# Activations of a two-layer decoder kernel stored as even and odd token rows, read in turn by every product

## The chip, the cores and the metric

The kernel runs on one core of a Trainium2 chip. The metric is the device time of one execution in microseconds (us); lower is better. Shown times of the kernel before are the median of three runs; the profile is of one more execution, with a time of its own.

## The reference

Two layers of a decoder on 272 tokens (16 learned meta tokens and 256 of the sequence), width 2048. Cut to what matters:

```python
def hybrid_layer(h, pos, norm_g, w_in, conv_w, conv_b, gn_g, w_branch, w_out):
    u = rms_norm(h, norm_g)
    proj = jnp.einsum('bld,de->ble', u, w_in)            # 2048 -> 18432 columns
    q, k, v, g_ret, c_x, c_pre, c_post, g_conv, m_ret, m_conv = split_columns(proj)
    ...
    y_ret = head_group_norm(retention_chunkwise(q, k, v), gn_g)
    y_ret = jnp.einsum('blc,cd->bld', y_ret * silu(g_ret), w_branch[0])
    z = causal_depthwise_conv(c_pre * c_x, conv_w, conv_b)
    y_conv = jnp.einsum('blc,cd->bld', (c_post * z) * silu(g_conv), w_branch[1])
    merged = sigmoid(m_ret) * y_ret + sigmoid(m_conv) * y_conv
    return h + jnp.einsum('bld,de->ble', merged, w_out)
```

All of it is float32. The 16 meta tokens are dropped after the last norm.

## The kernel before

Activations stand transposed: 128 partitions hold 128 channels, and tokens run along the free dimension. A vector of 2048 channels is 16 such pieces (`KC`, index `k`). A product of float32 accuracy is made of fp32r products: every weight `w` and every activation `a` is split into a high part and the rest (`wh`, `wl`, and the two rows of `act`), and `wh*ah + wh*al + wl*ah` is summed in PSUM.

The two activation tiles are `pair[0]` and `pair[1]` (`act` in the trace; lines 65, 384), 16 pieces times two rows (high, low) of 272 floats, 1088 bytes a row. They are written by `gain_input` (lines 168 to 173, the norm's gain), and by `split_act` (lines 154 to 158), always with one ACT instruction for the high row and one DVE instruction for the low row. They are read by TensorE alone, as the moving operand, in `product` (lines 124 to 151) and in the opening (line 478).

The work is a list of blocks, one per 128 output channels: 128 columns of a weight matrix against all 16 pieces of `u` or `y`. SP loads a block's weights two blocks ahead in two halves of 512 KB; ACT writes `wh` (line 117) and DVE `wl` (line 118) from them. The order of the blocks is the order in which the program lists them: in each layer 8 retention heads (6 blocks each), 16 merge gates, 16 blocks of `w_br[0]`, 16 convolution groups of 4, 16 merge gates, 16 of `w_br[1]`, 16 of `w_out`. The first four blocks are computed together in the opening, while the input arrives.

`product` has two forms. In layer 0 all 272 tokens are needed, and a piece takes three matmuls of 272 columns (line 148). In layer 1 most blocks need 256 tokens: high and low rows fit into one PSUM bank side by side, so a piece takes one matmul of 512 columns for `wh` (line 133) and one of 256 for `wl` (line 136), and ACT and DVE add the two halves (lines 141, 142). Some blocks of layer 1 stay in the first form, with 272 columns (keys and values) or 258 (the convolution inputs, which start two tokens early); the last block of all has it with 256.

```python
nc.tensor.matmul(
    both, wh[:, o:o + P], mov[:, k, :, c0:L], start=(k == 0), stop=False, skip_group_check=True
)
nc.tensor.matmul(
    ps[:, :n], wl[:, o:o + P], mov[:, k, 0, c0:L],
    start=False, stop=(k == KC - 1), skip_group_check=True,
)
```

Of the kernel before, what the change touches and what calls it, by code (L numbers as in the profile page):

```python
# [10 lines left out]
F32R = mybir.dt.float32r  # L11
# [7 lines left out]
L = SEQ + META  # L19
DEPTH = 2  # L20
P = 128
KC = D // P
# [23 lines left out]
def hybrid_trunk(ctx: ExitStack, tc: tile.TileContext, xT, w_first, w_in, w_br, w_out, gains, params, consts, dec, outT):  # L46
# [3 lines left out]
    act = ctx.enter_context(tc.tile_pool(name="act", bufs=1))  # L50
# [6 lines left out]
    def f32(t):  # L57
        return t.bitcast(F32)

    def new(name, cols=L):  # L60
        return tmp.tile([P, cols], F32, tag="t", name=name, padded_shape=[P, L])


    h = act.tile([P, KC, L], F32, name="h")
    pair = [act.tile([P, KC, 2, L], F32R, name=f"act{i}") for i in range(2)]
    ss = act.tile([P, L], F32, name="ss")
    sums = act.tile([P, 2, L], F32, name="sums")

# [23 lines left out]
    def norm_gain(layer, k):  # L92
        return gain[:, layer * KC + k:layer * KC + k + 1]
# [14 lines left out]
    def load(src, cols, queue=nc.sync):  # L108
        full = [P, HALF * P]
        raw = rawp.tile([P, cols], F32, name="raw", padded_shape=full)  # L110
        queue.dma_start(raw, src)
        wh = whp.tile([P, cols], F32R, name="wh", padded_shape=full)
        wl = wlp.tile([P, cols], F32R, name="wl", padded_shape=full)
        return raw, wh, wl

    def cut(raw, wh, wl):
        nc.scalar.copy(wh, raw)  # L117
        nc.vector.tensor_tensor(out=wl, in0=raw, in1=f32(wh), op=ALU.subtract)  # L118
        return wh, wl

    def split(src):
        return [cut(*load(src[:, j * HALF * P:(j + 1) * HALF * P], HALF * P)) for j in range(2)]

    def product(parts, mov, c0, spare=False, narrow=False):
        n = L - c0
        ps = psr.tile([P, 512], F32, name="pr") if spare else psm.tile([P, 512], F32, name="ps")
        if 2 * n <= 512 and not narrow:

            both = ps.rearrange("p (s n) -> p s n", s=2)
            for k in range(KC):  # L130
                wh, wl = parts[k // HALF]
                o = (k % HALF) * P
                nc.tensor.matmul(  # L133
                    both, wh[:, o:o + P], mov[:, k, :, c0:L], start=(k == 0), stop=False, skip_group_check=True
                )
                nc.tensor.matmul(  # L136
                    ps[:, :n], wl[:, o:o + P], mov[:, k, 0, c0:L],
                    start=False, stop=(k == KC - 1), skip_group_check=True,
                )
            b, a = new("pb", n), new("pa", n)  # L140
            nc.scalar.copy(b, ps[:, n:])  # L141
            nc.vector.tensor_tensor(out=a, in0=ps[:, :n], in1=b, op=ALU.add)  # L142
            return a
        for k in range(KC):
            wh, wl = parts[k // HALF]
            o = (k % HALF) * P
            for i, (w, m) in enumerate(((wh, 0), (wh, 1), (wl, 0))):
                nc.tensor.matmul(  # L148
                    ps[:, :n], w[:, o:o + P], mov[:, k, m, c0:L],
                    start=(k == 0 and i == 0), stop=(k == KC - 1 and i == 2),  # L150
                )
        return ps[:, :n]

    def split_act(dst, k, c0, src):

        hi, lo = dst[:, k, 0, c0:L], dst[:, k, 1, c0:L]
        nc.scalar.copy(hi, src)
        nc.vector.tensor_tensor(out=lo, in0=src, in1=f32(hi), op=ALU.subtract)  # L158

# [3 lines left out]
    def norm_input(layer, dst, k, c0):  # L163

        gain_input(layer, dst, k, c0)
        sum_squares(k, c0)

    def gain_input(layer, dst, k, c0):
        g = norm_gain(layer, k)
        hk = h[:, k, c0:L]  # L170
        hi, lo = dst[:, k, 0, c0:L], dst[:, k, 1, c0:L]
        nc.scalar.activation(hi, hk, AF.Copy, scale=g)
        nc.vector.scalar_tensor_tensor(out=lo, in0=hk, scalar=g, in1=f32(hi), op0=ALU.mult, op1=ALU.subtract)

# [50 lines left out]
    def retention(layer, hd, i0, u, y):  # L225
# [85 lines left out]
        def normed():  # L311
            ps = psr.tile([P, 512], F32, name="pr")[:, :L - i0]
            for i, part in enumerate(st["sq"]):
                nc.tensor.matmul(ps, onesr, part, start=(i == 0), stop=(i == 1))  # L314
            sd, rg = new("ysd", L - i0), new("rg", L - i0)
            nc.scalar.activation(sd, ps, AF.Sqrt, bias=eps)  # L316
            nc.vector.reciprocal(rg, sd)  # L317
            for c in range(2):
                a = new("yn", L - i0)
                tt(a, st["y", c], rg)  # L320
                tt(a, a, st["g", c])
                split_act(y, 2 * hd + c, i0, a)
# [24 lines left out]
    def conv(layer, k, i0, u, y):  # L347
# [30 lines left out]
        def cpost(ps):  # L378
            a = new("yc", L - i0)
            tt(a, ps, st["g"])  # L380
            split_act(y, k, i0, a)
# [9 lines left out]
    for layer in range(DEPTH):  # L391
# [23 lines left out]
        def merge(k):  # L415
            def done(ps, acc=acc, gm=gm, u=u, i0=i0):
                tt(gm[k], ps, gm[k])
                tt(acc[k], acc[k], gm[k], ALU.add)
                split_act(u, k, i0, acc[k])
            return done  # L420
# [31 lines left out]
    pss = [psm.tile([P, 512], F32, name="ps") for _ in range(FIRST)]  # L452
# [6 lines left out]
    for k0, nk in START:  # L459
        cols = FIRST * nk * P  # L460
        src = w_first[:, k0 * FIRST * P:(k0 + nk) * FIRST * P]
        ks = range(k0, k0 + nk)
        nc.sync.dma_start(h[:, k0:k0 + nk, :], xT[:, k0:k0 + nk, :])  # L463
        raw, wh, wl = load(src, cols, nc.sync if k0 else nc.scalar)
        if k0 == 0:
            nc.scalar.activation(warm, eps, AF.Sqrt)
            nc.vector.tensor_copy(wh, raw)
        for k in ks:
            gain_input(0, pair[0], k, 0)
        if k0 > 0:  # L470
            nc.scalar.copy(wh, raw)
        nc.vector.tensor_tensor(out=wl, in0=raw, in1=f32(wh), op=ALU.subtract)
        nc.scalar.activation(squares[:, k0:k0 + nk, :], h[:, k0:k0 + nk, :], AF.Square)
        for w, m in ((wh, 0), (wh, 1), (wl, 0)):
            for n in range(FIRST):
                for k in ks:
                    o = ((k - k0) * FIRST + n) * P
                    nc.tensor.matmul(  # L478
                        pss[n][:, :L], w[:, o:o + P], pair[0][:, k, m, :],
                        start=(k == 0 and w is wh and m == 0), stop=(k == KC - 1 and w is wl),  # L480
                    )
        if k0 == 2:
            for z in zp:
                nc.gpsimd.memset(z, 0.0)
# [4 lines left out]
    n = KC  # L489
# [9 lines left out]
    for b, (_, mov, c0, done) in list(enumerate(blocks))[FIRST:]:  # L499
        ps = product(ready.pop(b), mov, c0, spare=(b < FIRST + 2), narrow=(b == len(blocks) - 1))  # L500
        if b + 2 < len(blocks):
            ready[b + 2] = split(blocks[b + 2][0])
        if b == FIRST:
            layer_scales((sums[:, 0, :], sums[:, 1, :]))
            for i in range(FIRST):
                blocks[i][3](pss[i][:, :L])
        for fn in hooks.get(b, ()):
            fn()
        done(ps)
# [3 lines left out]
    for j in range(2):  # L513
        c = slice(META + j * half, META + (j + 1) * half)
        token_scale(c, (ss[:, c], sq[:, j * half:(j + 1) * half]))
        for i, (k, n, eng) in enumerate(FINAL):
            hk = h[:, k:k + n, c]
# [78 lines left out]
```

## Time and profile before

| | |
|---|---|
| median of three runs | 2325.72 us (2325.2 to 2325.87) |
| profiled execution: time | 2325.07 us |
| its span, first to last instruction | 2323.3 us |
| mean granted TensorE clock over the span | 0.998 |
| TensorE matmuls busy | 2308.6 us (99%), 16761 instructions |
| weight loads (PEld) busy | 2210.2 us (95%) |
| VectorE (DVE) busy | 1473.4 us (63%) |
| ScalarE (ACT) busy | 1061.8 us (46%) |
| read from HBM | 409.40 MB, 177 GB/s over the span |

The profiled execution's own time is 1.8 us over its span and 0.65 us under the median. A busy TensorE is not a TensorE at its peak: matmuls are pipelined, and the mean duration of one in the trace (287 ns for 272 columns) is longer than the distance from one to the next. What a matmul costs is read from the distance between starts, or from the length of a run of matmuls in the chain of work divided by their number.

### The profile page before, as it was taken

To read this page: it belongs to the slowest core of one execution; us is meant where nothing else is said; L and a number is where in the kernel's file an instruction comes from. 1 tells how busy PE (TensorE), PEld (TensorE's weight loads), DVE (VectorE), ACT (ScalarE), POOL (GpSimd) and SP (SyncE) were. 2 spreads that over 40 slices of the span, in tenths; PEclk is the share of its full clock that TensorE was granted. 3 is DMA by queue.
4 is the path that set the end of the run, shared out by engine and by line. 5 is a ranking of instruction groups with operands and counts; after the bars stand their busy time and mean duration, and the time that the engine had idled before them with its cause. 6 is when DMAs were issued, how large, how long until landed. Compare 5 with 4: busy or idle time off the path is not lost.

```text
span 2323.3 us, 40412 instructions
## 1 busy us (share of the span) xinstructions
PE 2308.6 (99%) x16761; PEld 2210.2 (95%) x16761; DVE 1473.4 (63%) x2046; ACT 1061.8 (46%) x1470; POOL 48.3 (2%) x52
## 2 busy tenths in 40 slices
PE   9999999999999999999999999999999999999997
PEld 9999999999999999999999999988899999988886
DVE  8767664446666565455667777755566666656765
ACT  6555553333333333444445555544444444444443
POOL 0000000000000000000100000000000000000012
PEclk9999999999999999999999999999999999999999
DMA  7555555555555555555555555455555555555553
GB/s 280 164 165 168 166 170 177 174 177 176 175 178 174 176 177 174 177 177 174 178 175 171 174 170 174 161 190 185 188 184 186 186 182 189 183 187 185 188 183 108
DMA packets 119177, 414.13 MB, mean 178 GB/s; under 512 B 13008, under 2 KB 19536, under 8 KB 118992
## 3 DMA queue, kind: packets, MB, share of 16 engines
q1 hardware_dynamic: 116224, 409.97, 54.4%
q8 instruction: 131, 2.15, 0.4%
q10 hardware_dynamic: 2768, 1.57, 0.2%
q14 instruction: 54, 0.44, 0.0%
HBM read 409.40 MB, written 2.10 MB: 177 GB/s over the span
## 4 chain that ended last, share of the span: by engine, by line
PE 99%; DVE 0%; DMA 0%; SPq 0%; ACT 0%; DVEq 0%; issue 0%; ACTq 0%
PE ps L148 62%; PE ps L133 22%; PE ps L136 11%; PE ps L478 1%; PE pr L223 1%; PE pr L300 1%; PE pr L148 1%; PE pr L280 0%; PE pr L268 0%; DMA raw<-in_w_first 0%; PE pr L314 0%; DVE h L519 0%; PE pr L197 0%; DVE rs L200 0%; DVEq L591 0%; SPq L463 0%
## 5 line engine op out<-in xcount | busy, mean ns | idle before, releaser
L148 PE MATMUL ps<-act,wh 128*128 128x272 f32 (+1 forms) x7776 | 1453.3, 287 | 0.0
L117 ACT CAST wh<-raw 128x1024 fp32r<-128x1024 f32 x760 | 798.7, 1051 | 1166.7 <-PE ps L148 557.6
L118 DVE TENSOR_TENSOR wl<-raw,wh 128x1024 fp32r<-128x1024 f32 x760 | 929.7, 1224 | 617.2 <-ACT wh L117 613.2
L148 PEld LDWEIGHTS ps<-act,wh 128*128 128x128 f32 x7776 | 1217.2, 188 | 0.8
L148 PE MATMUL ps<-act,wl 128*128 128x272 f32 (+1 forms) x3888 | 1118.0, 288 | 0.0
L133 PE MATMUL ps<-act,wh 128*128 128x512 f32 x2160 | 765.3, 395 | 0.0
L148 PEld LDWEIGHTS ps<-act,wl 128*128 128x128 f32 x3888 | 732.8, 188 | 0.0
L136 PE MATMUL ps<-act,wl 128*128 128x256 f32 x2160 | 611.8, 283 | 0.0
L133 PEld LDWEIGHTS ps<-act,wh 128*128 128x128 f32 x2160 | 405.6, 188 | 94.5 <-DVE act L158 0.3
L136 PEld LDWEIGHTS ps<-act,wl 128*128 128x128 f32 x2160 | 406.9, 188 | 0.1
L188 POOL TENSOR_TENSOR ss<-ss,sq 128x272 f32<-128x272 f32 (+1 forms) x28 | 32.7, 1166 | 1640.2 <-ACT sq L181 1640.2
L142 DVE TENSOR_TENSOR pa<-ps,pb 128x256 f32<-128x256 f32 x135 | 56.4, 418 | 5.0 <-ACT pb L141 5.0
L141 ACT COPY pb<-ps 128x256 f32<-128x256 f32 x135 | 49.4, 366 | 5.5 <-PE ps L136 5.5
L161 DVE TENSOR_TENSOR gs<-ps,rs 128x272 f32<-128x272 f32 x62 | 27.3, 440 | 35.9 <-PE ps L148 35.9
L317 DVE RECIPROCAL rg<-ysd 128x272 f32<-128x272 f32 (+1 forms) x16 | 28.9, 1803 | 8.5 <-ACT ysd L316 8.5
L364 DVE SCALAR_TENSOR_TENSOR cz<-zp,par,cz 128x272 f32<-128x272 f32 (+1 forms) x64 | 31.4, 490 | 1.1
L161 DVE TENSOR_TENSOR sgate<-ps,sgate 128x272 f32<-128x272 f32 x32 | 14.2, 442 | 25.4 <-PE ps L148 25.4
L161 DVE TENSOR_TENSOR gs<-pa,rs 128x256 f32<-128x256 f32 x64 | 27.1, 424 | 1.6
L161 DVE TENSOR_TENSOR zp<-ps,cx 128x272 f32<-128x272 f32 (+1 forms) x32 | 13.9, 435 | 22.4 <-PE ps L148 22.4
L344 ACT ACTIVATE sgate<-gs 128x272 f32<-128x272 f32 (+1 forms) x64 | 26.8, 418 | 0.0
L253 DVE SCALAR_TENSOR_TENSOR gt<-gs,par,sg 128x272 f32<-128x272 f32 (+1 forms) x32 | 15.8, 494 | 15.3 <-ACT sg L252 15.1
L308 POOL TENSOR_TENSOR ysq<-ysq 128x272 f32<-128x272 f32 (+1 forms) x16 | 12.2, 760 | 620.5 <-ACT ysq L305 544.2
(112 smaller groups left out, 880.2 us busy)
## 6 DMA issues: line engine op xcount, KB each, us to landing
raw<-in_w_in SPq DMA_DIRECT2D x568, 512.0 KB, 3.8
raw<-in_w_br SPq DMA_DIRECT2D x128, 512.0 KB, 3.7
raw<-in_w_out SPq DMA_DIRECT2D x64, 512.0 KB, 3.7
dec<-in_dec SPq DMA_DIRECT2D x16, 244.0 KB, 3.5
raw<-in_w_first SPq DMA_DIRECT2D x7, 512.0 KB, 7.6
h<-in_xT SPq DMA_DIRECT2D x7, 272.0 KB, 7.1
outT<-h ACTq DMA_DIRECT2D x2, 384.0 KB, 3.4
outT<-h SPq DMA_DIRECT2D x2, 256.0 KB, 2.3
```

The lines of the kernel that those rows point to most:

```text
L117: nc.scalar.copy(wh, raw)
L118: nc.vector.tensor_tensor(out=wl, in0=raw, in1=f32(wh), op=ALU.subtract)
L133: nc.tensor.matmul(both, wh[:, o:o + P], mov[:, k, :, c0:L], start=(k == 0), stop=False, skip_group_check=True)
L136: nc.tensor.matmul(ps[:, :n], wl[:, o:o + P], mov[:, k, 0, c0:L], start=False, stop=(k == KC - 1), skip_group_check=True,)
L141: nc.scalar.copy(b, ps[:, n:])
L142: nc.vector.tensor_tensor(out=a, in0=ps[:, :n], in1=b, op=ALU.add)
L148: nc.tensor.matmul(ps[:, :n], w[:, o:o + P], mov[:, k, m, c0:L], start=(k == 0 and i == 0), stop=(k == KC - 1 and i == 2),)
L161: nc.vector.tensor_tensor(out=out, in0=a, in1=b, op=op)
L188: nc.gpsimd.tensor_tensor(out=ss[:, c0:L], in0=ss[:, c0:L], in1=sq, op=ALU.add)
L317: nc.vector.reciprocal(rg, sd)
L344: nc.scalar.activation(s, g, AF.Sigmoid)
L364: nc.vector.scalar_tensor_tensor(out=a, in0=z[:, t + i0:t + L], scalar=conv_w(layer, k, t), in1=a, op0=ALU.mult, op1=ALU.add)
```

## The change

`pair` gets one more dimension: the tile `[128, 16, 2, 272]` (piece, high or low, token) becomes `[128, 16, 2, 2, 136]` (piece, even or odd, high or low, half the tokens). The even tokens of a piece (136 high values, then 136 low values) fill one row of 1088 bytes, the odd ones the next. Every reader and writer goes through both in turn: column 0 comes from the even row, column 1 from the odd row 1088 bytes on, column 2 from the even row again, 4 bytes on from column 0. The tile has the same size and place, PSUM is written in token order as before, and each product has as many columns as before.

```diff
-    pair = [act.tile([P, KC, 2, L], F32R, name=f"act{i}") for i in range(2)]
+
+    pair = [act.tile([P, KC, 2, 2, L // 2], F32R, name=f"act{i}") for i in range(2)]
...
+    def part(dst, k, m, c0):
+
+        return dst[:, k, :, m, c0 // 2:].rearrange("p e n -> p n e")
+
+    def turns(a):
+        return a.rearrange("p (n e) -> p n e", e=2)
...
-            both = ps.rearrange("p (s n) -> p s n", s=2)
+            both = ps.rearrange("p (m n e) -> p m n e", m=2, e=2)
...
-                    both, wh[:, o:o + P], mov[:, k, :, c0:L], start=(k == 0), stop=False, skip_group_check=True
+                    both, wh[:, o:o + P], mov[:, k, :, :, c0 // 2:].rearrange("p e m n -> p m n e"), start=(k == 0), stop=False, skip_group_check=True
...
-                    ps[:, :n], wl[:, o:o + P], mov[:, k, 0, c0:L],
+                    turns(ps[:, :n]), wl[:, o:o + P], part(mov, k, 0, c0),
...
-                    ps[:, :n], w[:, o:o + P], mov[:, k, m, c0:L],
+                    turns(ps[:, :n]), w[:, o:o + P], part(mov, k, m, c0),
...
     def split_act(dst, k, c0, src):
 
-        hi, lo = dst[:, k, 0, c0:L], dst[:, k, 1, c0:L]
+        hi, lo, src = part(dst, k, 0, c0), part(dst, k, 1, c0), turns(src)
...
-        hk = h[:, k, c0:L]
-        hi, lo = dst[:, k, 0, c0:L], dst[:, k, 1, c0:L]
+        hk = turns(h[:, k, c0:L])
+        hi, lo = part(dst, k, 0, c0), part(dst, k, 1, c0)
...
-                        pss[n][:, :L], w[:, o:o + P], pair[0][:, k, m, :],
+                        turns(pss[n][:, :L]), w[:, o:o + P], part(pair[0], k, m, 0),
```

No instruction is added, removed or moved on any engine, and no transfer changes. Waits stay where they were on DVE, ACT, POOL and SP. On PE a few of the waits for PE's own earlier results stand at other products: 72 of some 13,000 products have such a wait in the kernel before, 56 in the changed one.

## Rows read from the trace of the kernel before

**Rows 1.** The page's first two parts: engines; PE, DVE and granted clock by slice.
```profile
PE 2308.6 (99%) x16761; PEld 2210.2 (95%) x16761; DVE 1473.4 (63%) x2046; ACT 1061.8 (46%) x1470; POOL 48.3 (2%) x52
...
PE   9999999999999999999999999999999999999997
...
DVE  8767664446666565455667777755566666656765
...
PEclk9999999999999999999999999999999999999999
```

**Rows 2.** The page's fourth part: the chain that ended last, by engine.
```profile
PE 99%; DVE 0%; DMA 0%; SPq 0%; ACT 0%; DVEq 0%; issue 0%; ACTq 0%
```

**Rows 3.** The same chain in order of time: start, length, line, matmuls in a row.
```profile
328.93 864.01 PE ps L148 x6912
...
1673.71 11.47 PE ps L148 x96
...
2303.99 5.66 PE ps L148 x48
...
1217.91 0.66 PE pr L280 x6
```

**Rows 4.** Timeline of PE in layer 1: start, duration; first and last of 17.
```profile
1690.31 0.40 PE L133 MATMUL ps<-act,wh 128*128 128x512 f32 x1
...
1695.96 0.40 PE L133 MATMUL ps<-act,wh 128*128 128x512 f32 x1
```

**Rows 5.** Instructions by line and shape, PE: count, busy us, mean ns, idle before.
```profile
L148 PE MATMUL ps<-act,wh 128*128 128x272 f32 x6720 | 1263.5, 288 | 0.0
L148 PE MATMUL ps<-act,wl 128*128 128x272 f32 x3360 | 968.1, 288 | 0.0
L133 PE MATMUL ps<-act,wh 128*128 128x512 f32 x2160 | 765.3, 395 | 0.0
L136 PE MATMUL ps<-act,wl 128*128 128x256 f32 x2160 | 611.8, 283 | 0.0
L148 PE MATMUL ps<-act,wh 128*128 128x258 f32 x1024 | 184.1, 281 | 0.0
L148 PE MATMUL ps<-act,wl 128*128 128x258 f32 x512 | 145.4, 284 | 0.0
...
L280 PE MATMUL pr<-con,vT 128*72 128x128 f32 x64 | 9.6, 273 | 0.0
```

**Rows 6.** The same view: the writers of the activation tiles, ACT then DVE.
```profile
L172 ACT ACTIVATE act<-h,gain 128x272 fp32r<-128x272 f32 x32 | 15.8, 514 | 2.0 <-DMA h<-in_xT 1.9
L157 ACT CAST act<-sgate 128x272 fp32r<-128x272 f32 x16 | 6.7, 420 | 0.0
...
L173 DVE SCALAR_TENSOR_TENSOR act<-h,gain,act 128x272 fp32r<-128x272 f32 x32 | 22.5, 723 | 0.7 <-ACT act L172 0.7
L158 DVE TENSOR_TENSOR act<-sgate,act 128x272 fp32r<-128x272 f32 x16 | 6.9, 433 | 0.0
```

**Rows 7.** Busy us by stretch: PE, PEld, DVE, ACT, POOL; PEclk, DMA share, GB/s.
```profile
9.57:30.80 21.23, 21.23 (x170) 21.23 (x171) 19.85 (x25) 18.67 (x31) 0.00 (x0) 1.00 0.89 341
329.00:1192.00 863.00, 863.00 (x6906) 863.00 (x6905) 493.36 (x599) 347.15 (x407) 14.17 (x14) 1.00 0.55 176
```

**Rows 8.** Waits of the weight loads, all of them: total us, times, longest.
```profile
PEld pr L455 <- DVE eps L84: 1.4, 1, 1.4
PEld ps L478 <- ACT wh L471: 0.9, 1, 0.9
PEld pr L197 <- ACT sq L181: 0.8, 1, 0.8
PEld ps L133 <- DVE act L158: 0.3, 1, 0.3
PEld pr L223 <- ACT hi L217: 0.2, 1, 0.2
```

## Prediction

> **What bounds the kernel now.** I read the page's engine shares and slices first: TensorE is busy 99% of the span at full granted clock, DVE 63%, ACT 46% [rows 1]. Then the chain that ended last: 99% of it is PE [rows 2]. Then the waits: all that weight loads wait for comes to 3.6 us [rows 8]. So the time is the number of matmuls times the distance from one to the next, and the question is what sets that distance. The chain in order of time gives it, since its runs hold nothing but matmuls. 6912 matmuls of 272 columns take 864.01 us, 125.0 ns each; 96 of 258 columns take 11.47 us, 119.5 ns each; 48 of 256 columns take 5.66 us, 117.9 ns each [rows 3]. In layer 1, 16 pairs of a 512-column and a 256-column matmul take 1695.96 - 1690.31 = 5.65 us, 353.1 ns a pair [rows 4].
>
> The granted clock is 1.0 in these stretches [rows 7], that is 2.4 GHz. One column per cycle would be 113.3 ns for 272 columns, 107.5 for 258, 106.7 for 256 and 320.0 for the pair. The excess is 11.7, 12.0, 11.2 and 33.1 ns. It grows with the columns, not with the number of matmuls: the pair's two matmuls have three times the excess of one of 256 columns, as they have three times its columns. So a column takes 0.460 ns, not 0.417: the stream of activations itself runs 10% below the clock. The transposes of line 280 speak for the reading as the cause. They take 110.0 ns for 128 columns [rows 3], 0.833 ns a column (two cycles) and 3.3 ns over. At half the demand of bytes the excess per column is gone but for a small cost per matmul. And 258 columns, which start 8 bytes off a multiple of 16, cost 1.6 ns more than 256, where two more columns at 0.460 would be 0.9: it looks as if groups of four neighbouring columns, 16 bytes, are fetched, each in about 1.84 ns where the array wants it in 1.67, and a part of a group costs a whole one.
>
> **The change, part by part.** Instructions, their order, their columns and all transfers stay; only addresses change. Three things can move.
>
> *The reading.* Each row's group of four columns now lasts eight columns, 3.3 ns, and the stream asks in turn from two places. If the 0.17 ns that a group is late is the time to get the next group of the same row, two rows in turn hide it, and a column costs one cycle. No row shows a moving operand that hops, so the price is bounded: the low end of the time is one column per cycle and nothing per matmul; the high ends are the rivals B to D. I take one column per cycle plus a cost per matmul, between 0 and the 3.3 ns of the transposes, in the middle: 1.7 ns. Then:
> - 272 columns: 125.0 to 115.0, saves 10.0 ns; 6720 + 3360 [rows 5] and 96 in the two blocks behind the opening (16 pieces, three matmuls each), 10176 in all: 101.8 us.
> - 258 columns: 119.5 to 109.2, saves 10.3 ns; 1024 + 512 [rows 5]: 15.8 us.
> - pairs: 353.1 to 323.4, saves 29.7 ns; 2160 [rows 5]: 64.2 us.
> - the 48 of the last block: 117.9 to 108.4, 0.5 us.
>
> Together 182.3 us. The opening's 192 matmuls I leave out, since data sets their pace: transfers run at 341 GB/s there against 176 later [rows 7].
>
> [...]
>
> *The writing.* 128 ACT and 128 DVE instructions write the tiles in turns: 0.42 to 0.51 us each on ACT, 0.43 to 0.72 on DVE [rows 6]. A hopping write is bounded by nothing and by twice these: at most some 65 us more on DVE over the whole, 1540 of 2150 us. It lies under PE, as a whole block of 5.5 us or more stands between the last pieces written and their use: the last piece is read only by the last of 16 steps of the next block. The cover is thin in one place, the opening: DVE is busy 19.85 us of 21.23, ACT 18.67 [rows 7], and 16 gain writes stand there on each. Doubled by 0.5 us each they would cost 8 us; the nearest rows say nothing on hops, so I take 3 and keep 0 and 8.
>
> *What is late next.* Weight loads must follow: one every 115 or 109 ns. The transposes already run one load and one matmul each 110.0 ns [rows 3], so this is at the edge for 258 columns only, within the range. DVE's stretch of layer 0 is 493 us of 863 [rows 7]; ten per cent less time leaves it under 65%. The slices reach 8 tenths in retention [rows 1], so nearly full there, not over. PE's moved waits for itself stay under a few tenths of a us in all, taken as nothing: they name results that are blocks old.
>
> The sum: 2325.07 - 182.3 + 3 = 2145.8 us, on the profiled execution, 0.65 us under the median; **2146 us**. Its own range: with nothing per matmul the saving is 11.7 x 10176 + 12.0 x 1536 + 33.1 x 2160 ns + 0.5 = 209 us, 2116 us; with only half of the 182 us won back and 8 us in the opening, 2242 us.
>
> **The rivals.**
>
> *A, the forecast: the lateness of a group is hidden by the other row.* For it: the excess goes with bytes per time, not with instructions. Against: no row shows that two groups can be under way at once. 2116 to 2242 us.
>
> *B, the order does not matter.* The path to the array carries 16 bytes in 1.84 ns, wherever they come from, and both rows' groups are kept until used. Then as many groups pass as before: 2325 us, with the opening's cost up to 2333. For it: the excess is the same in all four shapes. Against: a pure limit of the path has no reason to sit 10% from the array's own rate.
>
> *C, a small loss: the two rows get into each other's way.* A group of the one row is asked for while that of the other is under way in the same place, and both are late. It decides as soon as a group is more than 3.3 ns away; a lateness twice that of now costs the excess once more, 209 us: 2327 to 2534 us. 1088 bytes is 68 groups, so the rows do not start alike, which speaks a little against it.
>
> *D, a fetch per column.* If only the last group is held, every column asks for its own. The least that this can cost is the transposes' two cycles a column: the 4.835 million columns (272 x 10176 + 258 x 1536 + 768 x 2160 + 256 x 48) take 4029 us, with 1.7 ns for each of 16080 matmuls 4057, against 2224 now (the four shapes' counts by their distances): 4158 us. If each fetch takes the 1.84 ns of a group, 8900 us are spent where 2224 were, and the time is about 9000 us. It decides if a second group isn't held, and for it speaks that a part of a group costs like a whole one. [...]
>
> **How the numbers follow.** A 0.55, B 0.12, C 0.13, D 0.20. The likeliest is A, 2146 us. A measurement of this kernel tells a change of over 0.2%, 4.7 us, from none. Faster is A, 0.55; B within 4.7 us, 0.10; slower is the rest of B with C and D, 0.35. The range leaves out D and no more: 2116 to 2534 us; A's own is 2116 to 2242.
>
> **What would show it.** Under A the chain's runs of 272 columns stand at 113 to 117 ns, those of 258 near 109, pairs near 323, while line 280 stays at 110. Under B the distances stay at 125.0 and 353.1. Under C they lie between 125 and 137. Under D they are 227 ns or more, DVE's share of the span falls to 35% or less, and the rest of the kernel stands idle around it. The writers' mean times show the price of hopping writes, the opening's length whether it counts. The forecast is wrong if the distance for 272 columns is over 121 ns, or if it falls and another engine ends the chain.

## The result, and the profile after

The changed kernel takes 2168.32 us (median of four runs, 2167.67 to 2170.3) against 2325.5 us (four runs of the kernel before): a ratio of 0.9325, 95% interval 0.9309 to 0.9342, 157 us or 6.7% less. Forecast were 2146 us, within 2116 to 2534. The profiled execution has a span of 2166.5 us and a time of 2168.32 us.

The page's first part, the granted clock by slice, and the chain that ended last, by engine, to set beside [rows 1] and [rows 2]:

```profile
PE 2147.9 (99%) x16761; PEld 2087.9 (96%) x16761; DVE 1493.0 (69%) x2046; ACT 1083.5 (50%) x1470; POOL 45.5 (2%) x52
...
PEclk9999999999999999999999999999999999999999
...
PE 4%; DVE 0%; DVEq 0%; ACT 0%; issue 0%; ACTq 0%
```

In this profile the chain is followed back over little more than the last 4% of the span, so that TensorE sets the time is read from its busy share and, below, from its waits. As many instructions as before, the same clock, TensorE again busy throughout: the matmuls themselves have moved closer together. How close shows in the busy time by stretch (stretch, then PE, PEld, DVE, ACT and POOL with their instructions, clock, DMA share, GB/s). The row below lies wholly in layer 0's long run of 272 columns:

```profile
320.00:1100.00 780.00, 780.00 (x6736) 780.00 (x6736) 487.99 (x582) 344.13 (x391) 10.69 (x13) 1.00 0.59 190
```

780 us over 6736 matmuls are 115.8 ns each, against 125.0 [rows 3]; 113.3 would be one column per cycle. The cycle in this is an estimate, since no row shows the clock other than as a share of full speed. In the chain of the kernel before stands, beside line 280 [rows 3], a run of four fp32 instructions of 272 columns:

```profile
1192.94 0.92 PE pr L197 x4
```

They take 230 ns each where the transposes of line 280 take 110.0 for 128 columns: 120 ns for 144 columns more, 0.833 ns a column. In the changed kernel a column takes 115.8/272 = 0.426 ns; with a cycle or more for each, 0.833 is two cycles or more. Taken as two, a cycle is 0.417 ns, the prediction's 2.4 GHz, and 272 columns are 113.3 ns.

For 258 columns I take the timeline of PE, two rows that are 30 matmuls apart (start, duration):

```profile
1582.48 0.39 PE L156 MATMUL ps<-act,wh 128*128 128x258 f32 x2
...
1585.83 0.39 PE L156 MATMUL ps<-act,wh 128*128 128x258 f32 x2
```

3.35 us over 30 are 111.7 ns, against 119.5 [rows 3]. The pairs and the last block stand in the chain in order of time (start, length); between the first two rows lie 33 pairs:

```profile
2074.48 0.22 PE ps L141
...
2085.29 0.22 PE ps L141
...
2147.51 5.37 PE ps L156 x48
```

A pair of a 512- and a 256-column matmul takes 10.81/33 = 327.6 ns against 353.1 [rows 4], a 256-column matmul of the last block 111.9 against 117.9. Times the counts of [rows 5] and of the prediction this is 9.2 x 10176 + 7.8 x 1536 + 25.5 x 2160 + 6 x 48 ns = 161 us. The profiled executions differ by 2325.07 - 2168.32 = 156.8 us; some 4 us were given back elsewhere. The same view of busy time by stretch says where (before, then after):

```profile
10.00:45.00 35.00, 35.00 (x279) 34.84 (x278) 31.09 (x39) 23.66 (x36) 0.00 (x0) 1.00 0.84 319
45.00:329.00 284.00, 283.97 (x2288) 283.71 (x2287) 201.01 (x323) 152.45 (x242) 6.21 (x8) 1.00 0.52 167
```
```profile
10.00:45.00 35.00, 32.30 (x268) 31.54 (x268) 31.51 (x36) 25.50 (x37) 0.00 (x0) 1.00 0.85 313
45.00:306.00 261.00, 260.26 (x2242) 259.81 (x2243) 200.51 (x322) 151.48 (x237) 5.33 (x7) 1.00 0.55 179
```

PE stands idle 2.7 us in the opening and just behind it, and 0.7 us in the rest of the retention stage, where it was idle 0.03 us before. What it waits for just behind the opening is new in the list of waits: a weight split of DVE (`wl`), and DVE's rotation of the keys (`k`).

```profile
PE ps L156 <- DVE k L169: 1.9, 1, 1.9
...
PE pr L156 <- DVE wl L119: 0.9, 1, 0.9
```

Both come later than in the kernel before, by the clock of the span and not only by PE's. In the opening ACT works without a gap once the input flows (busy in all of the 12.66 us from the first of the splits below before, of the 14.07 us after), and its weight splits mark the rounds. The rows are from the timelines, before, then after: two splits that are five rounds apart, and the rotation.

```profile
10.82 1.04 ACT L471 CAST wh<-raw 128x1024 fp32r<-128x1024 f32 x1
...
22.45 1.03 ACT L471 CAST wh<-raw 128x1024 fp32r<-128x1024 f32 x1
...
42.43 0.89 DVE L161 TENSOR_TENSOR k<-ps,sinr 64x272 f32<-64x272 f32 x2
```
```profile
11.73 1.02 ACT L479 CAST wh<-raw 128x1024 fp32r<-128x1024 f32 x1
...
24.77 1.03 ACT L479 CAST wh<-raw 128x1024 fp32r<-128x1024 f32 x1
...
44.31 0.89 DVE L169 TENSOR_TENSOR k<-ps,sinr 64x272 f32<-64x272 f32 x2
```

A round of ACT takes 2.61 us instead of 2.33, as two gain writes stand in each; the last split starts 2.3 us later than before, and the rotation 1.9 us. So the hopping writes lengthen the opening, and TensorE meets that just behind it. The steps between the last split and the rotation were not followed one by one.

The writers of the activation rows, beside [rows 6] (count, busy us, mean ns):

```profile
L181 DVE SCALAR_TENSOR_TENSOR act<-h,gain,act 128x272 fp32r<-128x272 f32 x32 | 28.3, 920 | 1.0 <-ACT act L180 0.9
L166 DVE TENSOR_TENSOR act<-sgate,act 128x272 fp32r<-128x272 f32 x16 | 10.1, 631 | 0.0
...
L180 ACT ACTIVATE act<-h,gain 128x272 fp32r<-128x272 f32 x32 | 23.4, 776 | 2.1 <-DMA h<-in_xT 2.1
L165 ACT CAST act<-sgate 128x272 fp32r<-128x272 f32 x16 | 11.0, 686 | 0.0
```

A hopping write costs 0.2 us more on DVE (433 to 631 ns) and 0.27 us on ACT (420 to 686). Over the whole DVE's busy time grows by 20 us (1473.4 to 1493.0) and ACT's by 22 us (1061.8 to 1083.5), hidden under PE but for the few us above.

### The profile page after: what moved, and what is told of

It reads as the page before. It is cut to its first block, busy times and chain, and to the rows that moved or that the text cites. A ratio compares the mean times of both kernels' runs of the same rounds, so it can differ in the third digit from the quotient of the medians.

```text
span 2166.5 us, 40399 instructions
## 1 busy us (share of the span) xinstructions
PE 2147.9 (99%) x16761; PEld 2087.9 (96%) x16761; DVE 1493.0 (69%) x2046; ACT 1083.5 (50%) x1470; POOL 45.5 (2%) x52
## 5 line engine op out<-in xcount | busy, mean ns | idle before, releaser
L156 PE MATMUL ps<-act,wh 128*128 128x272 f32 (+1 forms) x7776 | 1349.3, 279 | 1.9 <-DVE k L169 1.9
L156 PEld LDWEIGHTS ps<-act,wh 128*128 128x128 f32 x7776 | 1184.1, 189 | 2.6 <-ACT wh L118 2.1
L156 PE MATMUL ps<-act,wl 128*128 128x272 f32 (+1 forms) x3888 | 1082.6, 278 | 0.0
L141 PE MATMUL ps<-act,wh 128*128 128x512 f32 x2160 | 710.8, 382 | 0.3 <-DVE act L166 0.3
L144 PE MATMUL ps<-act,wl 128*128 128x256 f32 x2160 | 588.6, 273 | 0.0
L141 PEld LDWEIGHTS ps<-act,wh 128*128 128x128 f32 x2160 | 408.3, 189 | 56.4 <-DVE act L166 0.6
L181 DVE SCALAR_TENSOR_TENSOR act<-h,gain,act 128x272 fp32r<-128x272 f32 x32 | 28.3, 920 | 1.0 <-ACT act L180 0.9
```

The costliest lines, as they stand in the source:

```text
L141: nc.tensor.matmul(both, wh[:, o:o + P], mov[:, k, :, :, c0 // 2:].rearrange("p e m n -> p m n e"), start=(k == 0), stop=False, skip_group ...
L144: nc.tensor.matmul(turns(ps[:, :n]), wl[:, o:o + P], part(mov, k, 0, c0), start=False, stop=(k == KC - 1), skip_group_check=True,)
L156: nc.tensor.matmul(turns(ps[:, :n]), w[:, o:o + P], part(mov, k, m, c0), start=(k == 0 and i == 0), stop=(k == KC - 1 and i == 2),)
```

## Experiments: what about the reading makes it faster

Ten runs, each beside a run of the kernel before on the same chip (2324.5 to 2326.3 us). They give one time each. Read is above all the distance of 272-column matmuls in layer 0, from a row of the trace. Three theories at first: H, two groups of 16 bytes are held at once and last twice as long; P, the distance of the two rows matters; W, weight loads collide with the stream. The cuts of code show the lines that make the order; what else an experiment changes stands in its expectation.

**e1_544.** `pair` is `[P, KC, 2, 2, L // 2]` with high or low outside, even or odd inside:

```diff
-        return dst[:, k, :, m, c0 // 2:].rearrange("p e n -> p n e")
+        return dst[:, k, m, :, c0 // 2:].rearrange("p e n -> p n e")
...
```

> The even and odd rows stand 544 bytes apart instead of 1088; nothing else changes. Theory H (hold): the array's reader keeps two 16-byte groups at once, each lasts eight columns instead of four, and the lateness of a fetch is hidden whatever the two places are: 272 columns every 115 to 116 ns as in the changed kernel, time 2160 to 2180 us. Theory P (place): two groups are fetched side by side only if they lie in different places of the memory, and 1088 bytes (17 times 64) happens to be such a distance: at 544 bytes (8.5 times 64) some of the gain goes, 118 to 125 ns, 2200 to 2330 us. Theory W (weights): the 10% of before are collisions of the stream with the weight loads' reads, and going through two rows avoids them: any value between 115 and 125 ns, with matmuls of one shape unequal among themselves again.

**e2_17408.** All even rows, then all odd rows:

```diff
-    pair = [act.tile([P, KC, 2, 2, L // 2], F32R, name=f"act{i}") for i in range(2)]
+    pair = [act.tile([P, 2, KC, 2, L // 2], F32R, name=f"act{i}") for i in range(2)]
...
-        return dst[:, k, :, m, c0 // 2:].rearrange("p e n -> p n e")
+        return dst[:, :, k, m, c0 // 2:].rearrange("p e n -> p n e")
...
```

> The odd rows of all 16 pieces stand behind the even rows of all 16: 17408 bytes apart, a multiple of 1024. Theory H: 115 to 116 ns for 272 columns, 2160 to 2180 us. Theory P: the two rows agree in every address bit below 1024, so that two groups asked for together are in the same place: no gain or a loss, 125 ns or more, 2325 us or more. Theory W: as the starts of the rows relative to the weights now go through other values, between 115 and 125 ns.

Measured: 2168.41 and 2169.67 us. PE in the stretch from 600 to 1000 us, e1 then e2:

```profile
600.00:1000.00 400.00, 400.00 (x3456) 1.00 0.59 190
```
```profile
600.00:1000.00 400.00, 400.00 (x3455) 1.00 0.59 190
```

Both are 400 us over 3456 or 3455 matmuls, 115.7 or 115.8 ns, as with 1088 bytes. For two rows the distance has no part in it: P falls.

**e3_run4.** Four columns from the one row, then four from the other:

```diff
+    pair = [act.tile([P, KC, 2, 2, L // 8, 4], F32R, name=f"act{i}") for i in range(2)]
...
+        return dst[:, k, :, m, c0 // 8:].rearrange("p e n f -> p n e f")
...
-        if 2 * n <= 512 and not narrow:
+        if False:
...
-        z0 = max(i0 - 2, 0)
+        z0 = max(i0 - 8, 0)
```

> Two rows 1088 bytes apart as in the changed kernel, but four columns (16 bytes) are read from the one row before the other's four; layer 1 uses the form with three matmuls throughout (without the 512-column form), the convolution inputs of layer 1 start eight tokens early, and the low part of the norm's output is written by two instructions. So each group again lasts four columns, and successive groups come from two rows. Theory H: the gain comes from each group lasting eight columns, so it is gone: 125 ns for 272 columns, 118 for 256. Theory P: the gain comes from successive groups in different places, so it stays: 115 to 116 ns for 272, 112 for 256. Theory W: between the two. The whole time is not compared, since the blocks of layer 1 have another form; from distances alone it is some 2330 to 2390 us under H and 2190 to 2230 us under P.

Measured 2401.2 us; the long run of 272 columns in the chain:

```profile
338.28 890.88 PE ps L156 x6912
```

128.9 ns: the whole gain is gone, and 4 ns more. Two rows alone give nothing; each group must last. That is H's side, a little dearer than it said, and so is the whole time (2330 to 2390 us were named for H).

**e4_weights_128.** The kernel before, with `act.tile([P, 56], F32, name="gap")` for `[P, 24]`.

> The kernel before with its filler tile 128 bytes longer: the weight tiles start 128 bytes later relative to the activation rows, nothing else. Theories H and P: weights have no part in it, 125.0 ns for 272 columns, with the same spread of 121 to 128 ns in the same order, 2320 to 2331 us. Theory W: the collisions fall elsewhere, the mean or the order of the spread changes; a time 10 to 100 us away from 2325 us.

Measured 2325.02 us, and in the chain:

```profile
329.74 864.02 PE ps L148 x6912
```

125.0 ns, as before, but H was wrong on the order. From the starts in the trace, mean distances by place in the block run from 121 to 128 ns and repeat every four pieces; the three matmuls of piece 0 stand 126, 126 and 128 ns apart before, 123, 122 and 122 now, and the row of values has moved on by just one piece. So the place of the weights decides which matmul is late. Whether the weight loads are also what makes the matmuls late on the average, this run can't say. From one piece to the next the rows of activations move on by 2176 bytes and the weights by 512, that is by 128 bytes against each other beside a multiple of 512, and 512 bytes are four pieces: a shift by 128 bytes turns the pattern round and leaves its mean, under W too. W stays open as a reason for the lateness. What the other runs show of it: in the changed kernel and in e7 the spread is gone (115 or 116 ns for single matmuls of layer 0's long run).

**e5_run2, e6_8bytes, e7_16bytes.** Beside the form with three matmuls, which all of them have in layer 1, these three differ in `pair`, in the order in which `part` goes through it, and in where the convolution inputs start (the cuts are of e5, e6 and e7, in this order):

```diff
+    pair = [act.tile([P, KC, 2, 2, L // 4, 2], F32R, name=f"act{i}") for i in range(2)]
+        return dst[:, k, :, m, c0 // 4:].rearrange("p e n f -> p n e f")
...
+    pair = [act.tile([P, KC, 2, L // 4, 2, 2], F32R, name=f"act{i}") for i in range(2)]
+        return dst[:, k, m, c0 // 4:].rearrange("p n e f -> p n f e")
...
+    pair = [act.tile([P, KC, 2, L // 8, 2, 4], F32R, name=f"act{i}") for i in range(2)]
+        return dst[:, k, m, c0 // 8:].rearrange("p n e f -> p n f e")
```

> Two rows 1088 bytes apart, two columns (8 bytes) from the one, then two from the other; layer 1 in the three-matmul form throughout, the convolution inputs of layer 1 start four tokens early, the low part of the norm's output is written by two instructions. A 16-byte group still lasts eight columns, but every second column is the neighbour of the one before. Theory H (two groups held, each lasting eight columns): 115 to 116 ns for 272 columns, 111.7 for 256, as in the changed kernel; about 2185 to 2200 us. Theory C (collision: a column read right after its neighbour from the same group is what makes the stream late): half of the lateness is left, about 120 ns for 272 and 114 for 256, 2250 to 2290 us.

> All tokens of a piece in one row again, in an order in which successive columns stand 8 bytes apart within the same 16-byte group (places 0, 2, 1, 3 of each four); the rest as in e5_run2. A group lasts four columns, as before the change. Theory H: the gain is gone, 125 ns or more for 272 columns, 117.6 or more for 256; 2330 us or more. Theory C: no two neighbours in succession but the same group: if collisions are between neighbouring words alone, 115 to 116 ns; if within a group, 125.

> All tokens of a piece in one row, in an order in which columns come in turn from two neighbouring 16-byte groups (places 0, 4, 1, 5, 2, 6, 3, 7 of each eight); the convolution inputs of layer 1 start eight tokens early, the rest as in e5_run2. Each group lasts eight columns but its pair ends with it: after eight columns both are exhausted at once. Theory H, two groups held and fetched well ahead whatever their places: 115 to 116 ns for 272 columns, 111.7 for 256; 2185 to 2200 us. If the next group is asked for only as the last one is used up, the two are asked for right after each other: in part, 118 to 122 ns. Theory C: 115 to 116 ns.

Measured 3235.13, 2338.11 and 2185.68 us. The same run of the chain, of e5, e6 and e7:

```profile
446.55 1213.46 PE ps L156 x6912
```
```profile
328.83 864.01 PE ps L156 x6912
```
```profile
312.82 800.64 PE ps L156 x6912
```

175.6, 125.0 and 115.8 ns. The last two are as H says: hopping within a group gives nothing, and two neighbouring groups do as well as two distant rows. The first strikes both theories: two columns in a row from each of two rows are not as good as one (H) nor a little worse (the collision theory C of these expectations), but 40% slower than no hopping at all, though every group still lasts eight columns.

What tells e5 from the changed kernel is who comes back where. Take the odd and the even columns apart, as two lanes. In the changed kernel a lane stays in one row; in e5 each lane changes its row at every column; before, in e3 and in e6 a lane has two columns in a group and leaves it. That is theory L, put to two runs.

**e8_rows4, e9_step2.** Four rows in turn; and one row in steps of two words:

```diff
+    pair = [act.tile([P, KC, 4, 2, L // 4], F32R, name=f"act{i}") for i in range(2)]
+        return dst[:, k, :, m, c0 // 4:].rearrange("p e n -> p n e")
...
+    pair = [act.tile([P, KC, 2, L // 16, 8, 2], F32R, name=f"act{i}") for i in range(2)]
+        return dst[:, k, m, c0 // 16:].rearrange("p b n e -> p b e n")
```

> The changed kernel with four rows in turn instead of two: token 0 from the first row, 1 from the second, 2 from the third, 3 from the fourth, 4 from the first again, rows 544 bytes apart; the convolution inputs of layer 1 start four tokens early, the 512-column form stays. Theory H (groups are held until used up): each group now lasts 16 columns, 115 to 116 ns for 272 columns, 2165 to 2175 us. Theory L (lanes): even and odd columns are fetched by two lanes, each of which is late when its next column lies in another group than its last one; with two rows a lane stays in its row, with four it changes at every column, as in the runs of two columns: 170 to 180 ns for 272 columns, about 1.5 times before's distance less a tenth, 3000 to 3250 us.

> One row per piece; columns step by two words (8 bytes) through 64 bytes and then through the same 64 bytes one word on, so that the stream as a whole reads each 16-byte group twice in succession on a visit, and each group is visited twice. Layer 1 is in the three-matmul form, its convolution inputs begin with token 0. Theory H: a group lasts two columns and is fetched twice as often as before, 250 ns for 272 columns if each fetch takes 1.84 ns, 125 if two hits are enough. Theory L: each lane changes its group at every column, 170 to 180 ns for 272 columns and some 165 for 256; 3150 to 3300 us.

Measured 2688.39 and 4704.73 us:

```profile
376.43 1002.24 PE ps L156 x6912
```
```profile
636.54 1774.08 PE ps L156 x6912
```

145.0 and 256.7 ns. L has the sign of e8 against H, but neither size; for e9 it is H's first price that comes near, 250 ns, from 1.84 ns for each fetch. Counted in a lane's columns (136 of 272), e9 takes 1.89 ns each, every one in a new group; before the change it is 1.84 ns for each group of two, in e3 1.90. So, if there are such lanes, one needs an estimated 1.84 to 1.90 ns to come by a new group, however little it takes from it. Suppose that a lane holds two groups and fetches one at a time, and that a column already held takes 0.83 ns (a hit: a lane has every second column, so twice the 0.417 estimated above). While a lane uses only one group, the next is fetched into the free place meanwhile, and a group costs the longer of the two: the fetch before the change (1.84 ns against two hits), the hits in the changed kernel (four, 3.3 ns). Where a lane uses both groups by turns, no place is free, and fetches and hits add up. So a lane of e8 spends two fetches and six hits on eight columns, 17 x (2 x 1.85 + 6 x 0.83) = 148 ns, and of e5 two fetches and two hits on four, 34 x (2 x 1.85 + 2 x 0.83) = 182 ns; measured are 145.0 and 175.6. This is theory M, made to fit these runs; one more run tried it on something it had not seen.

**e10_rows8.** Eight rows in turn: `[P, KC, 8, 2, L // 8]`, else as e8.

> The changed kernel with eight rows in turn (272 bytes apart), the 512-column form kept, the convolution inputs of layer 1 starting eight tokens early. Theory M, made from the runs so far: even and odd columns are fetched by two lanes; each lane holds two 16-byte groups and fetches one at a time, some 1.8 to 1.9 ns each. With eight rows a lane goes round four groups, so with two held every column needs a fetch: 136 x 1.85 to 1.9 = 251 to 258 ns for 272 columns, 4550 to 4750 us. Rival R (a lane holds four groups or more, one fetch at a time): four fetches and twelve hits of 0.83 ns in sixteen columns of a lane, as dear per column as with four rows: about 145 ns, 2690 us. Theory H: 115 ns, 2170 us.

Measured 4329.3 us:

```profile
592.11 1635.84 PE ps L156 x6912
```

236.7 ns, 1.74 for each column of a lane. A fetch per column, as M says, against 145 for a lane that holds four groups: R and H fall. The size is 6 to 8% under M's 251 to 258 ns, outside its range, as the whole time is (4550 to 4750 us). With 1.74 ns for a fetch between distant rows, taken from this very run, the sums for e5 and e8 become 175 and 144 ns, on the measured ones; that a hop to another row fetches a little faster than a step to the next group was not asked of any run and stays open. Four and eight rows also stand closer together (544 and 272 bytes) than two; for these numbers of rows the distance was not varied, so that it has no part there is not shown. The lane itself stays open too: nothing in a trace shows it, it is a reading that fits all layouts to within some per cent.

## Why the prediction was right

**What bounds the kernel: right.** The time was the number of matmuls times their distance, and the excess over a column per cycle was one of reading: in layer 0's long run the same instructions in the same order run at 115.8, 125.0, 145.0, 175.6 or 256.7 ns as the addresses change alone.

**The mechanism: right for this layout, too simple as a rule.** The prediction held that a group is late because its 1.84 ns do not fit into the 1.67 ns of four columns, and that two groups in turn, each lasting eight columns, hide it. The changed kernel, e1, e2 and e7 agree (115.7 or 115.8 ns), and e3 and e6, whose groups last four columns, lose the gain (128.9 and 125.0). But in e5 each group of two rows lasts eight columns as well, and in e8 sixteen, and both are slower than the kernel before (175.6 and 145.0 against 125.0); by the prediction's rule they would have been as fast as the changed one. That the change took the one number of rows, and the one step, for which the rule holds is luck as far as the prediction goes. What the 1.84 ns are made of, a fetch alone or one that weight loads delay, no run shows.

**The size: 22 us too good**, in these terms:
- the cost per matmul, taken as 1.7 ns between 0 and 3.3, is 115.8 - 113.3 = 2.5 ns for 272 columns: 9.2 ns saved instead of 10.0, 8 us less.
- 258 columns came to 111.7 instead of 109.2 ns. In the three-matmul form 256 columns take as long (111.9), so columns don't set that distance. The weight loads, which the prediction had at the edge there, may be the floor, but that is not shown: in line 308 of the changed kernel the matmul behind one of 72 columns starts 61 to 78 ns after it, and the weight load behind the last of that line 108 to 110 ns after that load, but some loads of line 288 start 58 to 66 ns apart (all from the starts in the trace). No run took the loads away. 4 us less.
- a pair costs 7.6 ns over its columns, not 3.4: 25.5 saved instead of 29.7, 9 us less.
- the opening's 3 us came as some 3.4 us of idle PE, most of it right behind the opening, and, as far as the timelines show, mainly by the cause that was named: hopping gain writes, which make ACT's rounds 0.28 us longer.

**The writing: right**, 20 us of DVE within the bound of 65, under PE but for the opening's. The cover is thinner than was said: a block of layer 1, 16 pairs, lasts 5.2 us now, not 5.5; PE's wait for `act` is 0.3 us in all.

**The rivals.** B (order does not matter) fell with the result, C (two rows in each other's way) with it and with e1 and e2. D, a fetch per column, is no fantasy: by theory M it is what e9 and e10 do, and their 4705 and 4329 us are near its lower price of 4158. That it did not hold for two rows in turn is, by theory M, because a second group is held.

## What to carry to other kernels

Where TensorE is busy throughout at full clock, divide the distance of its matmuls by their columns before calling it the bound: 0.460 ns a column against the estimated 0.417 was 10%, of which the order of reading gave back most (9.2 of 11.7 ns for 272 columns). For a moving operand in fp32r, the type that these runs have, lay it out so that successive columns come in turn from two sequences, each read word by word; the two may be neighbouring 16-byte groups (115.8 ns in e7) or far apart (115.8 at 1088 bytes and at 17408), where plain rows take 125.0. Two columns at a time from each of two rows, or four rows, cost more than plain rows do (175.6 and 145.0 ns), and the writers pay some 0.2 to 0.3 us per row of 272 for the hops, so see that they have room, above all where all engines are full, as in the opening here.

## What the runs showed that was not expected

A write that hops after every two words costs hardly more than a plain one: in e5, with rows in runs of two, ACT's and DVE's writes, 442 and 436 ns, stay near the 420 and 433 of [rows 6], where the changed kernel's take 686 and 631 ns.

```profile
L165 ACT CAST act<-sgate 128x272 fp32r<-128x272 f32 x16 | 7.1, 442 | 0.6
...
L166 DVE TENSOR_TENSOR act<-sgate,act 128x272 fp32r<-128x272 f32 x16 | 7.0, 436 | 0.0
```

So an order that costs the writers almost nothing, two words at a time, is one of the worst for the reader, 175.6 ns against 125.0. And a matmul that only steps over every second word, all within the same 64 bytes, takes 256.7 ns for 272 columns, twice the distance of plain rows.
